# Batched softmax times V: one store a pass out of one result buffer, and the last passes' scores in other parts

## The chip, the cores and the metric

The kernel runs on one core of one Trainium2 chip. The metric is the device time of one execution in microseconds. Before the change three runs gave a median of 1061.16 us (1061.11 to 1061.69).

## What is computed

```python
"scores": np.random.randn(batch, n_heads, seq, seq)      # 8, 12, 1024, 1024, float32
"v":      np.random.randn(batch, n_heads, seq, head_dim) # 8, 12, 1024, 64, float32

scores_max = np.max(scores, axis=-1, keepdims=True)
attn = np.exp(scores - scores_max)
attn = attn / (np.sum(attn, axis=-1, keepdims=True) + 1e-8)
return np.matmul(attn, v)
```

There are 96 heads. For each, 1024 x 1024 scores are turned into weights row by row and multiplied by a 1024 x 64 matrix. The scores are 403 MB, V and the result 25 MB each.

## The kernel before

**Passes.** Four heads make a pass, and 24 passes are one loop (L477). A pass has two halves (`k` = 0 and 1) of two heads each. In a half the 128 partitions hold 2 x 64 groups of 16 consecutive rows of scores: partition x holds rows 0 to 15 of its group, 4 KB a row, so that a half is one [128, 16, 1024] float32 buffer (`s_bufs[k]`, 8 MB), and "a row" below means one row on each of the 128 partitions, 512 KB. V of the four heads is one 1 MB buffer, `v_sb`.

**A row's way.** ScalarE takes the exponential of two rows at a time (L431, one row at a time for the last four of the second half) into one of six `p_nat` buffers, in float16 and without subtracting the maximum. TensorE turns the row in eight 128 x 128 transposes (L444) into PSUM (`psT`, two buffers), VectorE copies two rows (L456, or one, L452) into `pt` (two buffers), and TensorE multiplies with V and a column of ones in eight matmuls (L164), three rows behind the transposes (`LAG`). The order on TensorE is written out by hand (`in_line`): transposes of row r, then products of row r - 3. After every three rows VectorE takes the reciprocal of the column of ones (L143) and multiplies (L151) into `out_bufs[k]`, [128, 16, 64] float32, 512 KB. GpSimd spreads V with ones into `vones` (L289) for each half and copies the finished results of both halves from `out_bufs` into two further buffers, `done` (`put_by`, L182), from which they are stored a pass later. ScalarE also watches V for size (L301), VectorE gathers the smallest and largest sums (L319, L320), and at the very end a judgement (L328 to L340) says whether the sums stayed in range; if not, a slow general path (L342) would do everything anew. With these inputs it isn't taken.

**SyncE's queue.** All transfers of the loop are issued on SyncE, in an order fixed by hand (`queue`). After the last transposes of a pass's first half, `load_first` (L255) issues for the next pass V (L277), the stores of the pass before (`store_before`, L187, one DMA for each half, L193; in passes 0 and 22 their condition is false, and pass 23 takes another branch), and the scores of the first half (L249). These go in one DMA of 8 MB, in the last two loads in parts of 4, 6 and 6 rows. After the whole pass `last` (L386) issues the scores of the second half, one DMA, or in the last two loads parts of 4, 2, 2, 2, 2, 2, 1 and 1 rows. Scores are loaded into the buffer that the same half of the current pass has just freed, so an issue waits on the exponentials that read it. A DMA is also held back until an earlier DMA that counts on the same semaphore has landed. Passes are counted from 0; the loads for passes 22 and 23 are the ones in parts.

**The last results.** There is no pass behind the last to store its results. In the last pass (23), `load_first` stores pass 21 from `done` and pass 22 from V's buffer (`spare`: in pass 22 `put_by` copies there, after V has been read), four DMAs of 512 KB through `store_last` (L206, L210); then `end` (L216) stores the last pass straight from `out_bufs`, in DMAs of 512, 384 and 128 KB, the last one for rows 12 to 15 of the second half.

Of the kernel before, what the change touches and what calls it, by code (L numbers as in the profile page):

```python
# [8 lines left out]
FP32 = mybir.dt.float32  # L9
# [17 lines left out]
def kernel(  # L27
# [6 lines left out]
    nc = tc.nc  # L34
    P = 128

    B, H, SQ, SK = scores.shape
    Bv, Hv, SKv, D = v.shape
    assert (B, H, SK) == (Bv, Hv, SKv)
    BH = B * H  # L40
# [5 lines left out]
    AHEAD = 4  # L46
# [6 lines left out]
    T = 2  # L53
    K = AHEAD // T
    W = P // T
    R = SQ // W
    PASSES = BH // AHEAD
# [8 lines left out]
    out_rows = out.rearrange("b h (j r) d -> (b h j) (r d)", j=W)  # L66

    const_pool = ctx.enter_context(tc.tile_pool(name="const", bufs=1))
    sb_pool = ctx.enter_context(tc.tile_pool(name="sbpool", bufs=1))
# [10 lines left out]
    def buffers(pool, count, shape, dtype, name):  # L80
        return [pool.tile(shape, dtype, name=f"{name}{k}") for k in range(count)]

    s_bufs = buffers(sb_pool, K, [P, R, SK], FP32, "s_nat")
    v_sb = sb_pool.tile([P, C // L, S, L, D], FP32, name="v_sb")
    p_bufs = buffers(sb_pool, 6, [P, EB, SK], FP16, "p_nat")
    pt_bufs = buffers(sb_pool, 2, [P, EB, SK], FP16, "pt")
    out_bufs = buffers(sb_pool, K, [P, R, D], FP32, "out_sb")
    done_bufs = buffers(sb_pool, K, [P, R, D], FP32, "done")
    small_pool = ctx.enter_context(tc.tile_pool(name="small", bufs=1))
    seen = small_pool.tile([P, 1 + K * R + 2], FP32, name="seen")  # L90
    nc.gpsimd.memset(seen, 1.0)
# [1 line left out]


    psO_bufs = buffers(ps_pool, 4, [P, 512], FP32, "psO")
    for buf in done_bufs:
        nc.vector.memset(buf, 0.0)  # L97
    cell = small_pool.tile([P, 1], FP32, name="cell")
    nc.vector.memset(cell, 0.0)
    done = [buf[:].rearrange("x r d -> x (r d)") for buf in done_bufs]  # L100
    spare = [
        v_sb[:].rearrange("x h s l d -> x (h s l d)")[:, k * R * D : (k + 1) * R * D]
        for k in range(K)
    ]
    turn = {}

    def take(bufs):
# [23 lines left out]
    def queue(dma):  # L131

        if queued:
            after(dma, queued[-1])
        queued.append(dma)
# [42 lines left out]
    def put_by(homes):  # L178

        for k in range(K):  # L180
            fills.append(
                nc.gpsimd.tensor_copy(  # L182
                    out=homes[k], in_=out_bufs[k][:].rearrange("x r d -> x (r d)")
                )
            )

    def store_before(m):  # L187

        before = (m + (PASSES - 1)) % PASSES
        for k in range(K):  # L190
            to = out_rows.rearrange("(m x) y -> m x y", x=P)[bass.ds(before * K + k, 1)]
            send(
                nc.sync.dma_start(  # L193
                    out=to.rearrange("o x y -> (o x) y"), in_=done[k], cond=(before < PASSES - 3)
                )
            )

    def send(dma):
        for other in stores:
            apart(dma, other)  # L200
            apart(other, dma)
        apart(dma, dma)
        stores.append(dma)
        queue(dma)

    def store_last(parts):  # L206

        for ago, k, home, a, b in parts:
            n = BH - ago * AHEAD + T * k
            store = nc.sync.dma_start(  # L210
                out=out_rows[n * W : (n + T) * W, a * D : b * D], in_=home[:, a * D : b * D]
            )
            ends.append(store)
            send(store)

    def end():  # L216

        cut = (GROUPS - 2) * G
        left = [out_bufs[k][:].rearrange("x r d -> x (r d)") for k in range(K)]
        store_last(((1, 0, left[0], 0, R), (1, 1, left[1], 0, cut), (1, 1, left[1], cut, R)))  # L220

    stores, fills, ends = [], [], []
    writers, users = {}, {}

    def apart(a, b, reason="stores of two heads are disjoint"):
        tc.declare_no_dep(a.ins, b.ins, across_iterations=True, reason=reason)
# [18 lines left out]
    def load(k, m, parts=(R,), r=0, **cond):  # L245
        rows_n = sc_rows[bass.ds(m * K + k, 1)].rearrange("o x r k -> (o x) r k")
        for rows in parts:
            queue(
                nc.sync.dma_start(  # L249
                    out=s_bufs[k][:, r : r + rows, :], in_=rows_n[:, r : r + rows, :], **cond  # L250
                )
            )
            r += rows

    def load_first(m):  # L255


        before = queued[-1:]
        n = (m + 1) % PASSES
        with tc.If(m < PASSES - 1) as cmp:  # L260
            load_v(n)
            store_before(m)
            then = queued[-1:]
            with tc.If(m < PASSES - 3) as cmp2:
                load(0, n)
            with cmp2.Else():
                queued[:] = then
                load(0, n, (4, 6, 6))
        with cmp.Else():
            queued[:] = before  # L270
            store_last([(3, k, done[k], 0, R) for k in range(K)])
            store_last([(2, k, spare[k], 0, R) for k in range(K)])

    def load_v(m, **cond):

        rows = v_bh.rearrange("(m x) y -> m x y", x=P)
        dma = nc.sync.dma_start(  # L277
            out=v_sb[:].rearrange("x h s l d -> x (h s l d)"),
            in_=rows[bass.ds(m, 1)].rearrange("o x y -> (o x) y"),
            **cond,  # L280
        )
        fills.append(dma)
        queue(dma)

    def spread_v(k):

        for t in range(T):
            for s in range(S):
                op = nc.gpsimd.tensor_copy(  # L289
                    out=vones[s * Q : (s + 1) * Q, k, :, t, 0:D].rearrange(  # L290
                        "i (h l) d -> i h l d", l=L
                    ),
                    in_=v_sb[(k * T + t) * Q : (k * T + t + 1) * Q, :, s],
                )
        return op

    def watch_v():


        junk = p_bufs[-1][:].rearrange("p r k -> p (r k)")  # L300
        return nc.scalar.activation(  # L301
            out=junk,
            in_=v_sb[:].rearrange("p h s l d -> p (h s l d)"),
            func=mybir.ActivationFunctionType.Abs,
            scale=1.0 / SUM_MAX,
            accum_out=seen[:, K * R + 1 : K * R + 2],
        )
# [8 lines left out]
    def fold():  # L316

        n = K * R + 1
        nc.vector.tensor_reduce(out=seen[:, 0:1], in_=seen[:, 0 : n + 1], axis=X, op=ALU.min)  # L319
        nc.vector.tensor_reduce(  # L320
            out=seen[:, n + 1 : n + 2], in_=seen[:, 1 : n + 2], axis=X, op=ALU.max
        )

    def judge(bank):

        n = K * R + 1
        part = small("part")
        nc.vector.tensor_scalar(  # L328
            out=part, in0=seen[:, n + 1 : n + 2], scalar1=1.0, scalar2=None, op0=ALU.is_le
        )  # L330
        nc.vector.scalar_tensor_tensor(  # L331
            out=right, in0=seen[:, 0:1], scalar=1.0 / SUM_MAX, in1=part, op0=ALU.is_ge, op1=ALU.mult
        )
        cell = bank[0:1, G * M : G * M + 1]
        in_line(
            nc.tensor.matmul(  # L336
                out=cell, lhsT=right[:], rhs=vones[:, 0, 0, 0, D : D + 1], start=True, stop=True
            )
        )
        nc.vector.tensor_copy(out=count[:], in_=cell)  # L340
# [45 lines left out]
    def last(m, bank):  # L386

        before = queued[-1:]
        k = K - 1
        with tc.If(m < PASSES - 1) as cmp:  # L390
            spread = spread_v(k)
            watch = watch_v()
            n = (m + 1) % PASSES
            with tc.If(m < PASSES - 3) as cmp2:  # L394
                put_by(done)
                queued[:] = before
                load(k, n)
            with cmp2.Else():
                with tc.If(m < PASSES - 2) as cmp3:
                    put_by(done)  # L400
                with cmp3.Else():
                    gate = nc.gpsimd.tensor_copy(out=cell, in_=out_bufs[k][:, R - 1, D - 1 : D])
                    for op in (watch, spread):
                        tc.add_manual_dep(
                            gate.ins,
                            op.ins.name,
                            mybir.DependencyInfo(
                                mybir.DependencyClass.Sync, mybir.DependencyReason.DATA
                            ),
                            reason="the values have been read",  # L410
                        )
                    put_by(spare)
                queued[:] = before
                load(k, n, (4, 2, 2, 2, 2, 2, 1, 1))
        with cmp.Else():
            queued[:] = before
            end()
            fold()
            judge(bank)

    def heads(m):

        for k in range(K):
            st = dict(psO=[take(psO_bufs) for g in range(GROUPS)])
            for r in range(R):
# [32 lines left out]
                if r == R - 1 and k < K - 1:  # L458
                    load_first(m)
# [58 lines left out]
```

## Time and profile before

| | |
|---|---|
| median of three runs | 1061.16 us (1061.11 to 1061.69) |
| the profiled execution | 1061.0 us |
| its span, first to last instruction | 1057.2 us |
| mean granted clock of TensorE | 0.889 |
| PE / PEld / DVE / ACT / POOL busy | 77 / 74 / 67 / 71 / 27% |
| read from HBM, written to it | 427.82 MB, 27.26 MB |
| chain that ended last | DMA of scores 7% of the span, other steps 1% and less |

PE is TensorE's matmuls, PEld its weight loads, DVE VectorE, ACT ScalarE, POOL GpSimd, SP SyncE; a q behind a name means the engine's sequencer, which issues and waits. A row of the page's groups names line, engine, operation, output and inputs with shapes and count, then busy us and mean ns of one, then idle time of the engine just before and what ended it. A row of a timeline has start in us from the span's start, length in us, engine, line, operation, tiles and count, and in brackets the idle time before. A row of windows has the stretch and its length, then the busy us of PE, PEld, DVE, ACT and POOL with their counts, then the granted clock of TensorE (1.00 is full), the mean busy share of the 16 DMA engines, and GB/s. The share can pass 1 a little, since packets overlap.

### The profile page before, as it was taken

What the parts mean: (1) busy time and instruction counts of PE and PEld (TensorE: products, weight loads), DVE (VectorE), ACT (ScalarE), POOL (GpSimd) and SP (SyncE); (2) the same over time, 40 slices, a digit from 0 to 9 for tenths busy, and PEclk for the clock granted to TensorE, in tenths of its full rate; (3) what the DMA queues carried; (4) which work ended last, traced back from release to release, by engine and by line L of the source; (5) the groups of instructions that cost most, each with busy time, mean ns of one, the idle gap of its engine ahead of it and who ended that gap; (6) DMA issues with size and microseconds to landing.
All of it is one profiled execution on the core that took longest, in us unless ns stands there. A gap on an engine that the chain in (4) does not pass through costs nothing. (4 is left out here: it accounts for less than half of the span.)

```text
span 1057.2 us, 32536 instructions
## 1 busy us (share of the span) xinstructions
PE 814.0 (77%) x12289; PEld 779.1 (74%) x12289; DVE 705.7 (67%) x1352; ACT 749.8 (71%) x482; POOL 286.6 (27%) x447
## 2 busy tenths in 40 slices
PE   3488668786787867878778777887777886878987
PEld 2488668785787867867678767787677876878877
DVE  2377566685676856767567675676656766667878
ACT  4487578776787667876778667786687856878965
POOL 4041231312323124121241221412214123131241
PEclk9799888898888988989889897898988889889999
DMA  9999999999999999999999999999999999999998
GB/s 397 438 437 429 404 454 427 426 431 426 447 436 436 436 431 441 422 436 427 423 435 436 436 436 436 436 436 412 446 434 429 422 430 443 436 436 420 424 429 322
DMA packets 20164, 453.06 MB, mean 429 GB/s; under 512 B 2240, under 2 KB 2368, under 8 KB 9024
## 3 DMA queue, kind: packets, MB, share of 16 engines
q1 hardware_dynamic: 20160, 452.99, 99.7%
q8 instruction: 4, 0.07, 0.0%
HBM read 427.82 MB, written 27.26 MB: 430 GB/s over the span
## 5 line engine op out<-in xcount | busy, mean ns | idle before, releaser
L431 ACT ACTIVATE p_nat<-s_nat 128x2048 f16<-128x2048 f32 (+1 forms) x432 | 702.7, 1711 | 291.6 <-SPq L394 159.6
L444 PE MATMUL psT<-ident,p_nat 128*128 128x128 f16 x6144 | 521.1, 236 | 214.0 <-ACT p_nat L431 212.7
L456 DVE COPY pt<-psT 128x2048 f16<-128x2048 f16 x336 | 411.3, 1224 | 310.3 <-PE L444 151.2
L444 PEld LDWEIGHTS <-p_nat 128*128 128x128 f16 x6144 | 436.5, 120 | 228.6 <-ACT p_nat L431 225.9
L164 PE MATMUL psO<-vones,pt 128*128 128x130 f16 x6144 | 499.1, 227 | 23.9 <-DVE pt L452 10.7
L289 POOL CAST vones<-v_sb 32x512 f16<-32x512 f32 x392 | 239.1, 610 | 761.2 <-PE L444 393.0
L164 PEld LDWEIGHTS <-pt 128*128 128x128 f16 x6144 | 400.6, 101 | 43.9 <-DVE pt L456 24.5
L151 DVE TENSOR_TENSOR out_sb<-psO,seen 64x192 f32<-64x192 f32 (+1 forms) x576 | 192.0, 333 | 22.1
L452 DVE COPY pt<-psT 128x1024 f16<-128x1024 f16 x96 | 63.4, 682 | 1.5
L143 DVE RECIPROCAL seen<-psO 128x3 f32<-128x3 f32 (+1 forms) x288 | 49.7, 173 | 11.9 <-PE L444 7.5
L301 ACT ACTIVATE p_nat<-v_sb 128x2048 f16<-128x2048 f32 x24 | 45.7, 1903 | 0.7 <-DMA v_sb<-in_v_dram 0.7
L182 POOL COPY done<-out_sb 128x1024 f32<-128x1024 f32 x44 | 44.5, 1037 | 4.8 <-issue 4.8
L301 ACT ACT_TABLE_LOAD x1 | 1.3, 1283 | 5.7 <-DMA v_sb<-in_v_dram 5.7
L319 DVE TENSOR_REDUCE seen<-seen 128x1 f32<-128x34 f32 x25 | 4.7, 189 | 0.8
L301 ACT ACTIVATION_READ_ACCUMULATOR p_nat<-v_sb 128x1 f32 x24 | 4.5, 189 | 0.0
L320 DVE TENSOR_REDUCE seen<-seen 128x1 f32<-128x34 f32 x25 | 4.5, 179 | 0.0
L97 DVE MEMSET done<- 128x1024 f32 x2 | 1.8, 912 | 1.2 <-DVEq L477 1.0
L182 POOL COPY v_sb<-out_sb 128x1024 f32<-128x1024 f32 x2 | 2.0, 1040 | 0.0
L336 PE MATMUL psO<-vones,right 128*1 128x1 f16 x1 | 0.2, 164 | 1.7 <-DVE right L331 1.7
L336 PEld LDWEIGHTS <-right 128*1 128x1 f16 x1 | 0.1, 79 | 1.9 <-DVE right L331 1.9
L340 DVE CAST count<-psO 1x1 int32<-1x1 f32 x1 | 0.1, 146 | 0.3 <-PE psO L336 0.3
masks.py:199 POOL TENSOR_SCALAR_AFFINE_SELECT ident<-ident 128x128 f32<-128x128 f32 x1 | 0.3, 295 | 0.1
(12 smaller groups left out, 1.8 us busy)
## 6 DMA issues: line engine op xcount, KB each, us to landing
v_sb<-in_v_dram SPq DMA_DIRECT2D x24, 1024.0 KB, 17.0
out_dram<-done SPq DMA_DIRECT2D x48, 512.0 KB, 12.0
s_nat<-in_scores_dram SPq DMA_DIRECT2D x4, 3072.0 KB, 24.4
s_nat<-in_scores_dram SPq DMA_DIRECT2D x10, 1024.0 KB, 27.7
s_nat<-in_scores_dram SPq DMA_DIRECT2D x2, 4096.0 KB, 18.7
s_nat<-in_scores_dram SPq DMA_DIRECT2D x4, 2048.0 KB, 23.3
s_nat<-in_scores_dram SPq DMA_DIRECT2D x4, 512.0 KB, 23.0
out_dram<-v_sb SPq DMA_DIRECT2D x2, 512.0 KB, 7.8
```

Source lines behind the costliest of these rows:

```text
L143: nc.vector.reciprocal(out=recip, in_=psO[:, :, D : D + 1])
L151: norm = nc.vector.tensor_tensor(out=out_bufs[k][part, g * G : g * G + rows, :], in0=psO[part, :, t * N : t * N + D], in1=recip[part].to_b ...
L164: product = nc.tensor.matmul(out=st["psO"][g][:, i * M : (i + 1) * M], lhsT=pt[:, c * P : (c + 1) * P], rhs=vones[:, k, c].rearrange("p t ...
L182: nc.gpsimd.tensor_copy(out=homes[k], in_=out_bufs[k][:].rearrange("x r d -> x (r d)"))
L289: op = nc.gpsimd.tensor_copy(out=vones[s * Q : (s + 1) * Q, k, :, t, 0:D].rearrange("i (h l) d -> i h l d", l=L), in_=v_sb[(k * T + t) * Q ...
L301: return nc.scalar.activation(out=junk, in_=v_sb[:].rearrange("p h s l d -> p (h s l d)"), func=mybir.ActivationFunctionType.Abs, scale=1. ...
L319: nc.vector.tensor_reduce(out=seen[:, 0:1], in_=seen[:, 0 : n + 1], axis=X, op=ALU.min)
L320: nc.vector.tensor_reduce(out=seen[:, n + 1 : n + 2], in_=seen[:, 1 : n + 2], axis=X, op=ALU.max)
L431: exp = nc.scalar.activation(out=p_nat[:, g : g + rows, :].rearrange("p r (x v) -> p x r v", v=Q * L), in_=s_bufs[k][:, r + g : r + g + ro ...
L444: turned = nc.tensor.transpose(out=psT[:, c * P : (c + 1) * P], in_=p_row[:, c // L, c % L, :], identity=ident16[:],)
L452: copy = nc.vector.tensor_copy(out=pt, in_=psT)
L456: copy = nc.vector.tensor_copy(out=pt2[:], in_=psT2[:])
```

## The change

The two `done` buffers become one tile, [128, 2, 1024] float32; GpSimd's copies go to its two halves, and a pass's results leave by one DMA of 1 MB that names for each partition two pieces of 4 KB, one in each half's rows of the result. The copies of pass 22 into V's buffer are addressed in the same manner. In the last pass the results of passes 21 and 22 leave by one DMA each instead of two; the three stores of the last pass stay as they are. The scores of the first half for passes 22 and 23 come in parts of 8, 4 and 4 rows, those of the second half in 4, 4, 2, 2, 2, 1 and 1. The description of the change adds that SyncE's program then has 187 words.

```diff
-    done_bufs = buffers(sb_pool, K, [P, R, D], FP32, "done")
+    done = sb_pool.tile([P, K, R * D], FP32, name="done")
...
-    for buf in done_bufs:
-        nc.vector.memset(buf, 0.0)
+    for k in range(K):
+        nc.vector.memset(done[:, k], 0.0)
...
-    done = [buf[:].rearrange("x r d -> x (r d)") for buf in done_bufs]
-    spare = [
-        v_sb[:].rearrange("x h s l d -> x (h s l d)")[:, k * R * D : (k + 1) * R * D]
-        for k in range(K)
-    ]
+    spare = v_sb[:].rearrange("x h s l d -> x (h s l d)").rearrange("x (k y) -> x k y", k=K)
...
-                    out=homes[k], in_=out_bufs[k][:].rearrange("x r d -> x (r d)")
+                    out=homes[:, k], in_=out_bufs[k][:].rearrange("x r d -> x (r d)")
...
+    def of_pass(m):
+
+        rows = out_rows.rearrange("(m k x) y -> m x k y", k=K, x=P)
+        return rows[bass.ds(m, 1)].rearrange("o x k y -> (o x) k y")
+
     def store_before(m):
 
         before = (m + (PASSES - 1)) % PASSES
-        for k in range(K):
-            to = out_rows.rearrange("(m x) y -> m x y", x=P)[bass.ds(before * K + k, 1)]
-            send(
-                nc.sync.dma_start(
-                    out=to.rearrange("o x y -> (o x) y"), in_=done[k], cond=(before < PASSES - 3)
-                )
-            )
+        send(nc.sync.dma_start(out=of_pass(before), in_=done[:], cond=(before < PASSES - 3)))
...
-    def store_last(parts):
-
-        for ago, k, home, a, b in parts:
-            n = BH - ago * AHEAD + T * k
-            store = nc.sync.dma_start(
-                out=out_rows[n * W : (n + T) * W, a * D : b * D], in_=home[:, a * D : b * D]
-            )
-            ends.append(store)
-            send(store)
+    def store_last(to, rows):
+        store = nc.sync.dma_start(out=to, in_=rows)
+        ends.append(store)
+        send(store)
...
-        left = [out_bufs[k][:].rearrange("x r d -> x (r d)") for k in range(K)]
-        store_last(((1, 0, left[0], 0, R), (1, 1, left[1], 0, cut), (1, 1, left[1], cut, R)))
+        for k, a, b in ((0, 0, R), (1, 0, cut), (1, cut, R)):
+            n = BH - AHEAD + T * k
+            store_last(
+                out_rows[n * W : (n + T) * W, a * D : b * D],
+                out_bufs[k][:, a:b, :].rearrange("x r d -> x (r d)"),
+            )
...
-                load(0, n, (4, 6, 6))
+                load(0, n, (8, 4, 4))
...
-            store_last([(3, k, done[k], 0, R) for k in range(K)])
-            store_last([(2, k, spare[k], 0, R) for k in range(K)])
+            store_last(of_pass(PASSES - 3), done[:])
+            store_last(of_pass(PASSES - 2), spare)
...
-                load(k, n, (4, 2, 2, 2, 2, 2, 1, 1))
+                load(k, n, (4, 4, 2, 2, 2, 1, 1))
```

## The prediction

> **What bounds the kernel now.** I read the page first: time, DMA, queues.
>
> ```profile
> span 1057.2 us, 32536 instructions
> ...
> DMA packets 20164, 453.06 MB, mean 429 GB/s; under 512 B 2240, under 2 KB 2368, under 8 KB 9024
> ...
> q1 hardware_dynamic: 20160, 452.99, 99.7%
> q8 instruction: 4, 0.07, 0.0%
> ```
>
> The 16 DMA engines are taken 99.7% of the span, while no compute engine of the page passes 77%. The 2240 packets under 512 B are 16 for each of 140 landed DMAs: each DMA ends with one small packet per engine. Then the stretches that no first or last pass touches, in windows, and the issues of two passes on SyncE:
>
> ```profile
> 104.00:940.00 836.00, 652.17 (x9786) 624.49 (x9783) 561.12 (x1077) 592.10 (x380) 225.80 (x346) 0.88 1.00 433
> ```
>
> ```profile
> 204.69 0.33 SPq L277 DMA_DIRECT2D v_sb<-in_v_dram  x1
> ...
> 859.51 0.33 SPq L277 DMA_DIRECT2D v_sb<-in_v_dram  x1
> ```
>
> Share 1.00 over 836 us: the transfers never stop. The two loads of V are 15 passes apart, so a pass takes 654.82 / 15 = 43.65 us. It moves 2 x 8.389 MB of scores, 1.049 MB of V and 1.049 MB of results, 18.87 MB.
>
> So only the end can bend. There, the timelines of ScalarE, TensorE and SyncE over the last pass:
>
> ```profile
> 1011.64 3.72 ACT L431 ACTIVATE p_nat<-s_nat 128x2048 f16<-128x2048 f32 x2 [2.91 <-PE psT L444]
> 1018.89 5.52 ACT L431 ACTIVATE p_nat<-s_nat 128x2048 f16<-128x2048 f32 x3 [3.53 <-PE L164]
> 1026.12 16.56 ACT L431 ACTIVATE p_nat<-s_nat 128x2048 f16<-128x2048 f32 x9 [1.72 <-DMA s_nat<-in_scores_dram]
> 1043.93 3.91 ACT L431 ACTIVATE p_nat<-s_nat 128x1024 f16<-128x1024 f32 x4 [1.24 <-PE L444]
> ```
>
> ```profile
> 1014.42 0.63 PE L164 MATMUL psO<-vones,pt 128*128 128x130 f16 x8 [0.45 <-DVE pt L452]
> 1016.21 1.95 PE L444 MATMUL psT<-ident,p_nat 128*128 128x128 f16 x32 [1.15 <-DVE out_sb L151]
> 1018.74 0.62 PE L164 MATMUL psO<-vones,pt 128*128 128x130 f16 x8 [0.58 <-DVE pt L456]
> 1020.86 0.64 PE L444 MATMUL psT<-ident,p_nat 128*128 128x128 f16 x8 [1.50 <-ACT p_nat L431]
> 1021.33 0.92 PE L164 MATMUL psO<-vones,pt 128*128 128x130 f16 x8
> ...
> 1028.09 0.64 PE L444 MATMUL psT<-ident,p_nat 128*128 128x128 f16 x8
> ...
> 1043.81 0.39 PE L444 MATMUL psT<-ident,p_nat 128*128 128x128 f16 x4
> ```
>
> ```profile
> 994.51 0.33 SPq L277 DMA_DIRECT2D v_sb<-in_v_dram  x1
> 996.88 2.56 SPq L193 DMA_DIRECT2D out_dram<-done  x2
> 1001.85 24.62 SPq L249 DMA_DIRECT2D s_nat<-in_scores_dram  x11
> 1035.93 2.75 SPq L210 DMA_DIRECT2D out_dram<-done  x2
> 1040.88 3.32 SPq L210 DMA_DIRECT2D out_dram<-v_sb  x2
> 1047.09 5.88 SPq L210 DMA_DIRECT2D out_dram<-out_sb  x3
> ```
>
> ScalarE starts at 1011.64, 1018.89 and 1026.12: the first half's parts of 4, 6 and 6 rows (2, 3 and 3 exponentials) arriving. The starts are 7.25 and 7.23 us apart, 6 rows each: **1.207 us a row**, 524288 B / 1.207 = 434.4 GB/s, so the first two are landings as well, whatever releaser the row names. From 1026.12 on nothing of the first half is missing, and the question is who is late. The windows with the granted clock:
>
> ```profile
> 1014.66:1018.07 3.41, 2.26 (x39) 2.04 (x36) 1.86 (x6) 0.69 (x1) 2.62 (x5) 1.00 0.99 425
> 1018.07:1021.49 3.42, 1.35 (x21) 1.11 (x20) 1.65 (x2) 2.60 (x2) 3.11 (x6) 1.00 1.07 460
> 1021.49:1024.90 3.41, 3.41 (x36) 3.41 (x33) 1.65 (x3) 2.92 (x2) 1.31 (x2) 0.50 0.93 401
> ...
> 1028.09:1051.73 23.64, 22.64 (x377) 21.52 (x376) 22.14 (x44) 18.41 (x12) 3.37 (x6) 1.00 0.97 389
> ```
>
> TensorE is busy 22.64 of the last 23.64 us, so **from row 10 of the first half on TensorE, with VectorE's copies, sets the end**, and the last data is not late: the last exponential ends at 1047.84, the last products only at 1051.7. From the transposes of row 10 at 1028.09 to those of row 26 at 1043.81 are 16 rows in 15.72 us, **0.98 us a row** against DMA's 1.207.
>
> **The change, part by part.** All against the profiled execution: 1061.0 us, 3.8 us of it outside the span. The median of the runs is 1061.16.
>
> *One store for two.* In passes 1 to 21 the two stores of 512 KB become one of 1 MB, at the end four become two, and the last scores' parts fall from 11 to 10 in two passes: 21 + 2 + 2 = 25 DMAs fewer, the same bytes. What a DMA costs by itself: at 434.4 GB/s a pass's 18.87 MB take 43.44 us of its 43.65, so all five DMAs of a pass together cost 0.21 us at most. A fifth of it, 0.04 us, is my upper guess for the average, 25 x 0.04 = 1.0 us; the lower end is 0. I take 0.3, nearer to none, since the bytes and most packets stay. If the second store alone carried all 0.21 us, the end would be 21 x 0.21 = 4.4 us earlier. It could also lose: a partition now reads two 4 KB pieces and writes them far apart; no row has such a store, and I bound that loss by the same 1.0 us. The second issue that goes from SyncE is hidden: its queue waits on the exponentials in any case (504 us below), and the copies into the buffer (two of 1.04 us on GpSimd) end long before the issue.
>
> *Counters and waits.* SyncE's waits:
>
> ```profile
> SPq L249 <- ACT p_nat L431: 504.3, 50, 26.4
> ...
> SPq L277 <- DMA s_nat<-in_scores_dram: 5.3, 1, 5.3
> ...
> SPq L193 <- DMA s_nat<-in_scores_dram: 3.5, 2, 1.9
> ```
>
> A load of V that waits 5.3 us for scores has no data reason: it shares a landing counter with an earlier part. Eight counters taken in turn by program order fit this. With one store and one part fewer, the counter of pass 22's V load passes from the part of rows 6 and 7 to that of rows 10 and 11, 4 x 1.207 = 4.8 us later, so it issues at 994.5 + 4.8 = 999.3. Behind it on SyncE stand the skipped store and all scores of the last pass. The work that hides it is DMA's own queue: V lands at 1018.89 - 10 x 1.207 = 1006.8, the last row of pass 22 (1.049 MB / 434.4 GB/s = 2.4 us) before it, at 1004.4, the last but one at 1003.2. With this last but one row's counter the first scores are issued at 1003.2 instead of 1001.85, 3.6 us before V is through. Once this cover is gone, each us late is a us lost.
>
> *Parts of 8, 4, 4.* Pass 22's scores: ScalarE is still busy with pass 21 when the 8 rows land, nothing moves. Last pass: the first exponential waits for 8 rows instead of 4, 1011.64 + 4 x 1.207 = 1016.47, less 0.3: 1016.2. It ends 1.90 later, at 1018.1; the following pairs end every (5.52 - 1.90) / 2 = 1.81 us, without the waits of 3.53 and 1.72. Rows 4 and 5 are ready at 1018.1 + 2 x 1.81 = 1021.7, and from there TensorE needs 0.98 a row: row 10 at 1027.6 (its exponential: 1018.1 + 5 x 1.81 = 1027.2, in time). Before it was 1028.09, so **0.5 us earlier, if the clock stays up**.
>
> It will hardly stay. In the window 1018.07 to 1021.49 TensorE was busy 1.35 of 3.42 us and the next window ran at clock 0.50; there a group of eight takes about 0.85 instead of 0.45 (1022.05 to 1022.90 the transposes). After the change TensorE has nothing from 1015.05 (1014.42 + 0.63) to 1018.1, then two rows, then waits again: a window that holds this is emptier still. If the slow window falls on 1018.07 to 1021.49, the first four rows end at 1021.6 and row 4 begins at 1022.05: 0.35 late, row 10 at 1028.0, 0.1 before now. If it begins near 1019.9, it holds 3.4 us of full work, which fills half the rows: up to 1.6 late, row 10 at 1029.2, 1.1 after now. The middle, 0.8 late, gives row 10 at 1028.4, **0.3 us later than now**. Before, the slow window lay ahead of ScalarE's gap of 1.72 us, which swallowed it; now there is no gap behind it. The Trainium skill ("TensorE: Matmul & The Clock Gate", Part 1: The HAM clock gate) says that about 3.4 us of idling put the array on half clock and about 3.4 us of work bring it back, in windows that run free of the program; these rows agree (3.41 us at 0.50), and without such a rule the part would be worth the 0.5 us.
>
> *Parts of 4, 4, 2, 2, 2, 1, 1.* Rows 4 and 5 of the second half now land with rows 6 and 7: 1026.12 + 8 x 1.207 - 0.3 = 1035.5, exponential done at 1037.4. TensorE comes to row 20 at 1028.4 + 10 x 0.98 = 1038.2: hidden by its backlog; if that went, at most 0.5 us appear.
>
> *The end.* After the last products come normalising, the judging and the last store, which all move with TensorE:
>
> ```profile
> L210 SPq DMA_DIRECT2D out_dram<-out_sb x3: 332/333/336, 1047.1 to 1052.6; - x3
> ```
>
> ```profile
> DMA to landing us min/median/max: 1.9/5.8/12.0
> ```
>
> Issued at 1052.6, landed 1.9 later, at 1054.5, with 2.7 us of closing behind. The merged stores of `done` and V's buffer queue behind the last scores as now, so DMA itself would be through some 0.3 us earlier, but the last store waits for VectorE. An end earlier by more than 0.7 us would meet the stores before it.
>
> *Words of SyncE.* Instruction packets by the DMA view of 24 to 60 us, and of 1056 us to the end:
>
> ```profile
> q8 instruction: 3, 0.05, 0.5%
> ```
>
> ```profile
> q8 instruction: 1, 0.02, 4.6%
> ```
>
> Three between 24 and 60 us, when SyncE stands in its longest wait (26.4 us) and TensorE goes through its long body for the first time, and one after 1056. So none of the three is SyncE's as I read them; the fourth comes after the last landing. I take 0; bounds 0 to 0.9 us gained (4.6% of 16 engines over 1.2 us).
>
> Sum: 1061.0 + 0.3 = **1061.3 us**.
>
> **The rivals.**
>
> 1. *The clock stays up or the data wins.* Row 10 0.5 us earlier, DMA saving up to 1.0 instead of 0.3: 1061.0 - 0.5 - 0.7 = 1059.8 at the far end, 1060.5 by the values taken. For it: ScalarE loses two gaps. Against: the idle stretch of 3 us.
> 2. *Slower: the clock stays down for two windows.* The mean clock of 0.88 over the middle puts (1 - 0.88) / 0.5 = 0.24 of every pass, 10 us or three windows, at 0.50. Two windows of 3.41 us, begun near 1019.9, hold rows 2 to 6 with their products; row 7 starts 2.9 us late, row 10 at 1030.5 against 1028.09: 2.4 later, 1063.4. Begun at 1018.07 they cost 1.3, 1062.3. It decides only if the first slow window finds too little work. Against: before, one busy window was enough to come back.
> 3. *Each store has a price of its own.* Then 21 of them go: at most 4.4 us by the rows, 1056.6. Against: share 1.00 and 433 GB/s with stores, 434.4 without. The Trainium skill ("DMA: Bandwidth & Descriptors", Rules for kernel authors and Anatomy of one DMA) asks for 1 MiB or more per DMA and fits a fixed cost of about 2.0 us each on another issuing path; by that 25 DMAs would be worth 50 us, an estimate from that page; the pass length here leaves no room for it.
> 4. *It does nothing.* The parts of the last pass are lost in TensorE's backlog and the stores in a full queue: 1061.0.
>
> **How the numbers follow.** A measurement of this kernel can tell about 0.2%, 2.1 us, from no change. Forecast 0.60 (1060.9 to 1062.1); rival 1 0.17, of it 0.05 beyond the bound by a dearer store; rival 2 0.13, of it 0.08 beyond, with the far loss of a store in two pieces added; rival 3 0.02; rival 4 0.08. Faster 0.05 + 0.02 = 0.07, slower 0.08, rounded up to 0.09 for what the counters may do, within 0.84. The range takes rival 1's far end and rival 2's: 1059.8 to 1063.4.
>
> **What would show it.** In the page after: 25 x 16 = 400 packets under 512 B fewer, a mean still near 429 GB/s. In ScalarE's timeline: one start near 1016.2 and no gap until the second half's data. In the windows: a stretch of clock 0.50 beginning between 1017 and 1020. Row 10's transposes near 1028.4, the last products about 0.3 after 1051.7. I am wrong if the pass is not 43.6 us, if the first scores of the last pass are issued after V has landed, or if the last products end with a gap of TensorE ahead of them.

## The result, and the profile after

The changed kernel took 1059.38 us (median of 22 runs, 1059.06 to 1059.73), the kernel before 1061.07 us (22 runs, 1060.39 to 1061.69). The ratio is 0.9985, with a 95% interval of 0.9979 to 0.9990: some 1.7 us faster, below the range of the prediction. The profiled execution took 1059.14 us.

First the page of after: span, packets, queues and the chain that ended last.

```profile
span 1057.4 us, 32323 instructions
...
DMA packets 19508, 453.06 MB, mean 428 GB/s; under 512 B 1840, under 2 KB 1968, under 8 KB 8624
...
q1 hardware_dynamic: 19504, 452.99, 99.6%
q8 instruction: 4, 0.07, 0.0%
...
PEld 3%; DVE 2%; PE 1%; POOL 0%; issue 0%; ACT 0%; PEldq 0%; POOLq 0%; ACTq 0%
```

**The span has not become shorter**: 1057.4 us against 1057.2. What became shorter is what lies outside it: 1061.0 - 1057.2 = 3.8 us before, 1059.14 - 1057.4 = 1.74 us after. The single runs say the same. Over the 22 runs of after the time outside the span is 1.79 us (1.71 to 1.88), over the 30 runs of before that stand beside the first four experiments 3.91 us (3.40 to 4.21). The span's median is 1057.6 (1057.3 to 1058.0) against 1057.15 (1056.9 to 1057.5). So the change **gains 2.1 us outside the span and loses 0.45 us inside it**.

What runs behind the span shows when a window of the DMA view is put there. Before, from 1057.2 to 1063 us (the second row is queue, packets, MB, share of 16 engines):

```profile
DMA packets 2, 0.02 MB, mean 3 GB/s; under 512 B 0, under 2 KB 0, under 8 KB 0
...
q14 instruction: 2, 0.02, 0.9%
```

After, from 1057.4 to 1063 us:

```profile
DMA packets 0, 0.00 MB, mean 0 GB/s; under 512 B 0, under 2 KB 0, under 8 KB 0
```

Before, two instruction packets of 8 KB come on queue 14 when every instruction that the trace shows has ended; by the trace's records they start at 1058.62 and 1060.80 us. After, none comes.

Inside the span, ScalarE's last pass (timeline of after; start, length, then the tiles, and in brackets the idle time before):

```profile
1016.04 18.33 ACT L425 ACTIVATE p_nat<-s_nat 128x2048 f16<-128x2048 f32 x10 [7.66 <-PE psO L160]
1035.45 9.40 ACT L425 ACTIVATE p_nat<-s_nat 128x2048 f16<-128x2048 f32 x6 [1.08 <-PE psT L438]
1045.15 1.06 ACT L425 ACTIVATE p_nat<-s_nat 128x1024 f16<-128x1024 f32 x1 [0.29 <-PE L438]
1046.66 1.06 ACT L425 ACTIVATE p_nat<-s_nat 128x1024 f16<-128x1024 f32 x1 [0.45 <-PE psT L438]
```

TensorE's timeline of after, with row 10 of the first half and the last products:

```profile
1018.00 1.08 PE L438 MATMUL psT<-ident,p_nat 128*128 128x128 f16 x16 [2.06 <-ACT p_nat L425]
1019.80 1.89 PE L438 MATMUL psT<-ident,p_nat 128*128 128x128 f16 x16 [0.72 <-ACT p_nat L425]
...
1028.08 0.61 PE L438 MATMUL psT<-ident,p_nat 128*128 128x128 f16 x8
...
1051.22 0.63 PE L160 MATMUL psO<-vones,pt 128*128 128x130 f16 x8 [0.45 <-DVE pt L446]
```

And the windows of after, with the granted clock in the third column from the right:

```profile
1014.66:1018.07 3.41, 0.90 (x13) 0.55 (x11) 2.00 (x7) 2.03 (x2) 1.81 (x3) 1.00 1.00 428
1018.07:1021.49 3.42, 2.70 (x32) 2.55 (x33) 1.23 (x1) 3.42 (x3) 3.05 (x5) 0.67 1.00 426
1021.49:1024.90 3.41, 3.41 (x53) 3.41 (x52) 2.00 (x2) 3.41 (x3) 2.15 (x3) 0.83 1.00 428
...
1028.09:1051.73 23.64, 22.43 (x379) 21.43 (x376) 22.14 (x44) 17.65 (x12) 2.25 (x4) 1.00 0.97 394
```

One exponential start replaces three, at 1016.04. The clock is down for (1 - 0.67) x 2 x 3.42 + (1 - 0.83) x 2 x 3.41 = 3.4 us, one stretch begun near 1019.2. Row 10 comes at 1028.08 and the last products at 1051.22, 0.12 later than before. The chain of before had shown no GpSimd at its end. In after GpSimd closes it (chain of after, its last pieces; start, length, what):

```profile
1048.48 0.82 PE psO L160 x15
1049.31 0.59 POOL vones L283
...
1053.98 0.61 POOL vones L283
```

These eight casts spread V into `vones` for a pass that doesn't exist; nobody reads their values. The row names TensorE's products as what released them, but the products that read this half of `vones` (the first half's) ended near 1037.1, some 12 us earlier, and the row of before names the transposes: what ends the wait is a landing. The POOL timelines of before, then of after:

```profile
1048.06 5.29 POOL L289 CAST vones<-v_sb 32x512 f16<-32x512 f32 x8 [25.26 <-PE L444]
```

```profile
1049.30 5.29 POOL L283 CAST vones<-v_sb 32x512 f16<-32x512 f32 x8 [25.64 <-PE psO L160]
```

The first store of `done` in the last pass stands in SyncE's order where other passes have the load of V, and by that order counts on the same landing counter. The DMA view at its issue (engine, KB, us from issue to landing), before with the issue at 1035.93, then after with the issue at 1040.42:

```profile
out_dram<-done SPq DMA_DIRECT2D x1, 512.0 KB, 12.0
```

```profile
out_dram<-done SPq DMA_DIRECT2D x1, 1024.0 KB, 8.7
```

1035.93 + 12.0 = 1047.9 and 1040.42 + 8.7 = 1049.1: in both kernels the casts begin within 0.2 us of that landing, and so they do in all twelve profiles (0.15 us behind it each time, by the trace's own times). The merged store is twice as long, lands 1.2 us later, and the casts end at 1053.98 + 0.61 = 1054.6 instead of some 1053.4.

### The profile page after: what moved, and what is told of

It is laid out like the page before. It is cut to its first block, busy times and chain, and to the rows that moved or that the text cites. A ratio compares the mean times of both kernels' runs of the same rounds, so it can differ in the third digit from the quotient of the medians.

```text
span 1057.4 us, 32323 instructions
## 1 busy us (share of the span) xinstructions
PE 814.7 (77%) x12289; PEld 779.7 (74%) x12289; DVE 705.6 (67%) x1352; ACT 749.6 (71%) x482; POOL 285.5 (27%) x447
```

## The experiments

Three theories. **Theory 1**: the time behind the span goes by the length of SyncE's program, whatever of it is carried out. Counted in the built programs (words of 64 B, branch labels left out) before has 206 words and after the 187 that the change names. The words of the other engines' programs were not counted. **Theory 2**, the rival: it goes by what is carried out, the 25 DMAs fewer or the other parts. **Theory 3**, for the span: the loss comes from GpSimd's casts, which wait for a longer store; its rival is TensorE's clock under parts of 8, 4, 4. All ratios are to before, with a 95% interval. Before had a median of 1061.05, 1061.11 and 1061.08 us beside the first four runs, the next four and the last two.

**Longer again, nothing more carried out.** Four scores loads stand in the loop of the general path, which these inputs never enter:

```diff
 # after, in the loop of general()
+            nc.sync.dma_start(out=s_bufs[0][:, 5, :], in_=s_rows[...])   # four times
```

> The changed kernel, with four loads on SyncE added to the general path, which is not entered with these inputs: every instruction that is executed stays, SyncE's program grows from 187 to 208 words (before the change 206). Theory 1, the gain is the length of SyncE's program, paid after the last instruction: the time outside the span goes back from about 1.8 to 3.8 us, the total from 1059.4 to about 1061.4, the span stays at 1057.6, and two 8 KB instruction packets appear behind the span. Theory 2, the gain is in what is executed (one store, fewer DMAs to close): outside the span 1.8 us, total 1059.4.

1061.57 us (10 runs), ratio 1.0006 (0.9996 to 1.0015): the whole gain is gone. The span is 1057.6 as in after, and 3.90 us (3.82 to 4.22) lie outside it. From 1057 to 1064 us the DMA view shows the two packets of queue 14 again (one of queue 8 comes near the end of every kernel here, changed or not):

```profile
q8 instruction: 1, 0.02, 1.0%
q14 instruction: 2, 0.02, 0.9%
```

Instructions that never run cost 2.1 us. That is theory 1, and theory 2 has no place for it.

The same profile also bears on theory 3. It carries out what after carries out, but TensorE is ahead in it:

```profile
1049.49 5.28 POOL L283 CAST vones<-v_sb 32x512 f16<-32x512 f32 x8 [26.90 <-PE psO L160]
```

```profile
1027.58 0.61 PE L442 MATMUL psT<-ident,p_nat 128*128 128x128 f16 x8
...
1050.73 0.63 PE L160 MATMUL psO<-vones,pt 128*128 128x130 f16 x8 [0.45 <-DVE pt L450]
```

Row 10 and the last products are 0.5 us earlier than in after, the last store lands at 1054.35 instead of 1054.62, and yet the span is 0.2 us longer: the casts began 0.2 us later. Here they alone hold the end.

**Shorter, all DMAs kept.** The kernel before without its general path, with 187 words on SyncE; every store and load of before is carried out. It leaves out the answer to sums out of range, and the branch that asks for it.

```diff
 # before
-    with tc.If(good < P, preferred_fallthrough_block=False):
-        general()
```

> The kernel before the change, with its stores and parts, but without the general path, so that a judgement of out of range would have no consequence; SyncE's program shrinks from 206 to 187 words, what is executed stays but for the jump over the path. Theory 1 (length of SyncE's program): outside the span 1.8 instead of 3.8 us, total about 1059.1. Theory 2 (what is executed, stores and DMAs): nothing gained, 3.8 us and 1061.1.

1058.38 us (9 runs), ratio 0.9975 (0.9965 to 0.9985). Outside the span 1.92 us (1.74 to 2.11); the span is 1056.5, some 0.6 shorter: the last store lands as before (1054.44 against 1054.51), and 2.1 us follow it instead of 2.7, with the branch gone. Without a single DMA less, the 2 us come.

**The new parts alone**, with the two stores of before:

```diff
 # before
-                load(0, n, (4, 6, 6))
+                load(0, n, (8, 4, 4))
...
-                load(k, n, (4, 2, 2, 2, 2, 2, 1, 1))
+                load(k, n, (4, 4, 2, 2, 2, 1, 1))
```

> The kernel before with the new parts of the last passes alone; two stores out of two buffers stay. SyncE's program has 195 words. Theory 1: the threshold lies somewhere from 188 to 206 words, so outside the span either 1.8 or 3.8 us and nothing between, which narrows it; span 1057.2 to 1057.7. Theory 2 (one store for two is what pays): 3.8 us and about 1061.3.

1059.86 us (10 runs), ratio 0.9988 (0.9978 to 0.9997). SyncE has 195 words, and 1.80 us lie outside the span: the parts alone already bring the program below the step. But the span is 1058.05, above the 1057.2 to 1057.7 expected and the longest median of all, and its runs scatter from 1057.0 to 1059.2.

**The change with the old first parts:**

```diff
 # after
-                load(0, n, (8, 4, 4))
+                load(0, n, (4, 6, 6))
```

> The changed kernel with the first half's parts of passes 22 and 23 back at 4, 6 and 6 rows; SyncE's program keeps its 187 words. If the forecast's step on the parts holds (8, 4, 4 costs some 0.3 us because TensorE's slow window has no gap behind it to swallow it), the span is 0.2 to 0.5 us shorter than the changed kernel's, about 1057.2, and the total about 1059.0. If the parts do nothing: 1059.4. If 8, 4, 4 is a gain: 1059.7 or more.

1059.27 us (10 runs), ratio 0.9984 (0.9974 to 0.9994); 187 words, 1.77 us outside, span 1057.45 (1057.3 to 1057.9). The span is 0.15 shorter than after's 1057.6, less than the 0.2 to 0.5 expected: with 8, 4, 4 taken away GpSimd is still there, its casts begin at 1049.31.

**The last store of `done` in two again**, for theory 3:

```diff
 # after
-            store_last(of_pass(PASSES - 3), done[:])
+            for k in range(K):
+                store_last(of_pass(PASSES - 3)[:, k], done[:, k])
```

> The changed kernel, but in the last pass alone the results of pass 21 leave by two stores of 512 KB again; 189 words on SyncE. Theory 3: the span's 0.4 us over the kernel before come from GpSimd, whose eight last casts (5.3 us, of V that nobody reads) wait for the first store of the last pass to land; 1 MB lands at 1049.2, 512 KB about 1.25 us earlier. By it the casts start near 1048.0, GpSimd is done at 1053.7 instead of 1054.9, the end falls back to the last store's landing, the span is 0.2 to 0.4 us shorter (about 1057.2), the total 1059.0 to 1059.2. If the 0.4 us come from the slow clock behind the first part of 8 rows, casts move and the span stays at 1057.6.

1059.55 us (10 runs), ratio 0.9985 (0.9976 to 0.9995), span 1057.75, from 1056.9 to 1059.5. The casts do move:

```profile
1048.66 5.29 POOL L284 CAST vones<-v_sb 32x512 f16<-32x512 f32 x8 [24.44 <-PE psT L439]
```

They begin 0.64 earlier than in after, though the last scores land 0.6 later in this execution (1047.19 against 1046.57); yet the median of the span isn't shorter. In the profiled execution TensorE was on half clock for two windows:

```profile
1018.07:1021.49 3.42, 2.13 (x26) 1.97 (x27) 1.22 (x1) 3.42 (x3) 3.12 (x6) 0.73 1.01 431
1021.49:1024.90 3.41, 3.41 (x35) 3.41 (x33) 1.23 (x1) 3.41 (x3) 2.60 (x4) 0.50 1.00 428
1024.90:1028.31 3.41, 3.41 (x50) 3.41 (x48) 2.23 (x5) 3.41 (x3) 0.00 (x0) 0.77 1.03 442
```

At half speed it spent 0.27 x 2 x 3.42 + 3.41 + 0.23 x 2 x 3.41 = 6.8 us, each window's lost share taken twice. Its rows:

```profile
1030.10 0.61 PE L439 MATMUL psT<-ident,p_nat 128*128 128x128 f16 x8
...
1053.28 0.64 PE L160 MATMUL psO<-vones,pt 128*128 128x130 f16 x8 [0.45 <-DVE pt L447]
```

Row 10 is 2.0 us later than before, the last products 2.2, the span 1059.2. Theory 3 is right about the casts, but alone it doesn't set the span.

**Both at once**, the split store and the old first parts (the two edits above together):

> As the split store, with the first half's parts at 4, 6 and 6 rows as before; 189 words. In the run with these parts alone the last store landed 0.4 us earlier than in the changed kernel, and only GpSimd's casts held the end. Theory 3: both gains add up, span 1056.7 to 1057.0, total 1058.5 to 1058.8, the fastest of all with the general path. If the parts do nothing: as the split store alone.

1059.02 us (10 runs), ratio 0.9979 (0.9969 to 0.9989), span 1057.2 (1056.7 to 1057.6). Against the version with the old first parts alone the casts begin 0.6 earlier and the span's median is 0.25 shorter, not quite the 1056.7 to 1057.0 expected.

**Where the step lies.** Three loads that are never carried out instead of four, 203 words:

> The changed kernel with three never executed loads on SyncE in the general path: 203 words. Theory 1: a threshold between 195 (fast) and 206 (slow); here either 1.8 us outside the span and 1059.4, or 3.9 us and 1061.5, nothing between.

1061.35 us (8 runs), ratio 1.0001 (0.9991 to 1.0011). Outside the span 3.44 us (3.29 to 3.56), between the two levels where nothing was expected, and one packet behind the span (DMA view, 1058.3 to 1064 us):

```profile
DMA packets 1, 0.01 MB, mean 1 GB/s; under 512 B 0, under 2 KB 0, under 8 KB 0
...
q14 instruction: 1, 0.01, 0.4%
```

**The one store alone**, all parts as before, 198 words:

```diff
 # after
-                load(0, n, (8, 4, 4))
+                load(0, n, (4, 6, 6))
...
-                load(k, n, (4, 4, 2, 2, 2, 1, 1))
+                load(k, n, (4, 2, 2, 2, 2, 2, 1, 1))
```

> The changed kernel with all the old parts (4, 6, 6 and 4, 2, 2, 2, 2, 2, 1, 1), so that one store for two is the only change; 198 words. Theory 1: 1.8 us outside the span if the threshold is above 198, else 3.9. Theory 3: the span is that of the changed kernel with old first parts, 1057.5, for the casts wait for the same 1 MB store; total 1059.3 or 1061.4.

1058.89 us (10 runs), ratio 0.9979 (0.9970 to 0.9989). Outside 1.79 us, no packet there; so 198 words are short enough. The span is 1057.05 (1056.9 to 1057.9), 0.25 below that of before beside it (1057.3), and 0.55 below the whole change: better than expected. The single runs of this version and of before overlap, so the 0.25 us is a small difference of medians.

**The one store alone, split again at the end**, 199 words:

> The change with all the old parts (4, 6, 6 and 4, 2, 2, 2, 2, 2, 1, 1) and with the last pass's store of done as two DMAs again; SyncE has 199 words. Theory 1 (length of SyncE's program, with the step between 198 and 203 words): time outside the span 1.8 us if the step lies above 199, 3.4 if it lies at 199. Theory 3 (GpSimd's casts of the last pass wait for the landing of the first store of done): casts start some 0.4 us earlier than in the version that only has the one store, 1048.1 against 1048.5; the span is shorter by at most 0.2 us than its 1057.05, since there the last store's landing already holds the end: 1056.9, time 1058.7. Rival: the split costs as much as it gives, time 1058.9 as in that version.

1058.75 us (11 runs), ratio 0.9979 (0.9970 to 0.9988), span 1057.0 (1056.6 to 1057.4), 1.78 us outside. The casts begin at 1047.89 instead of 1048.51, the span is the same within 0.1: here the last store ends last anyway, as expected. So there are two steps, one packet each: between 199 and 203 words, worth 1.65 us, and between 203 and 206, worth 0.45. It is the fastest version that keeps the general path, though the one before it isn't told apart from it.

**The first parts 8, 4, 4 with the old second parts**, 198 words:

```diff
 # after
-                load(k, n, (4, 4, 2, 2, 2, 1, 1))
+                load(k, n, (4, 2, 2, 2, 2, 2, 1, 1))
```

> The change with the old parts of the second half (4, 2, 2, 2, 2, 2, 1, 1) and the new parts of the first half (8, 4, 4); SyncE has 198 words, so time outside the span 1.8 us by theory 1. What it tells apart is where the 0.5 us of the span come from that the whole change has more (1057.6) than the version with the one store alone (1057.05). If 8, 4, 4 bring them (TensorE's half clock placed late), the span is 1057.4 to 1058 and scatters by a us or more, time 1059.2 to 1059.8. If 4, 4, 2, 2, 2, 1, 1 bring them (last scores issued later, first store of done landed later, GpSimd later), the span is 1057.0, time 1058.9.

1059.68 us (11 runs), ratio 0.9982 (0.9973 to 0.9991), 1.81 us outside, as expected if 8, 4, 4 cost the 0.5 us. The span is 1057.9 and falls in two groups: 1056.4, 1056.5, 1056.9 and 1057.1, and seven runs from 1057.5 to 1058.1. The profiled execution, one of 1058.1, in windows and in TensorE's timeline:

```profile
1014.66:1018.07 3.41, 0.42 (x8) 0.24 (x5) 1.18 (x5) 1.70 (x1) 2.60 (x5) 0.91 1.01 432
1018.07:1021.49 3.42, 3.15 (x29) 2.98 (x30) 1.22 (x1) 3.42 (x3) 3.11 (x6) 0.50 1.04 446
1021.49:1024.90 3.41, 3.41 (x40) 3.41 (x38) 1.23 (x2) 3.41 (x3) 1.31 (x2) 0.59 0.95 408
```

```profile
1018.34 3.70 PE L438 MATMUL psT<-ident,p_nat 128*128 128x128 f16 x32 [3.25 <-ACT p_nat L425]
...
1029.00 0.61 PE L438 MATMUL psT<-ident,p_nat 128*128 128x128 f16 x8
...
1052.15 0.64 PE L160 MATMUL psO<-vones,pt 128*128 128x130 f16 x8 [0.45 <-DVE pt L446]
```

The parts of 8, 4, 4 make TensorE idle 3.25 us, the clock is down for two windows (6.8 us), row 10 is 0.9 later and the last products 1.05 later than before. The same stretch in the version with the old parts and the split store:

```profile
1018.07:1021.49 3.42, 1.39 (x22) 1.25 (x23) 1.55 (x2) 2.73 (x2) 3.11 (x6) 1.00 1.03 446
1021.49:1024.90 3.41, 3.41 (x64) 3.41 (x62) 2.35 (x5) 2.79 (x2) 1.20 (x2) 1.00 1.00 430
```

There the clock stays up in this execution; in before it was down for one window, ahead of a gap of ScalarE that swallowed it.

**What decides between one slow window and two.** The clock's records in the traces change in steps of 3.41 us, and their edges lie elsewhere from execution to execution. With windows on these edges, first after, then the change with the last store in two again:

```profile
1015.81:1019.22 3.41, 1.22 (x19) 0.93 (x16) 0.95 (x5) 3.18 (x2) 2.89 (x5) 1.00 1.04 447
1019.22:1022.63 3.41, 2.83 (x27) 2.83 (x28) 2.09 (x2) 3.41 (x3) 3.10 (x7) 0.50 0.97 418
1022.63:1026.05 3.42, 3.42 (x63) 3.42 (x61) 2.12 (x5) 3.42 (x3) 1.03 (x2) 1.00 1.02 436
```

```profile
1016.23:1019.64 3.41, 1.25 (x21) 1.01 (x18) 1.01 (x5) 2.96 (x2) 2.76 (x5) 1.00 1.00 428
1019.64:1023.05 3.41, 2.69 (x27) 2.60 (x26) 1.89 (x2) 3.41 (x3) 3.10 (x6) 0.50 1.00 428
1023.05:1026.47 3.42, 3.42 (x35) 3.42 (x33) 1.21 (x2) 3.42 (x3) 1.17 (x2) 0.50 1.05 450
```

TensorE was busy 2.83 us of the slow window in the one, and the clock came back; 2.69 in the other, and it stayed down. The other kernels with 8, 4, 4 fit: one slow window with 3.08 us of work in it (208 words), two where the first held 2.65 (the new parts alone), 2.55 (8, 4, 4 with the old second parts) or none (203 words). Over all windows of the twelve traces up to 1050 us, the clock fell after 499 windows with at most 1.64 us of TensorE's work and stayed up after 2326 with at least 1.45; it came back after 487 with at least 2.64 and stayed down after 322 with at most 2.70. So in these traces it falls below some 1.5 us of work in 3.41 and returns above some 2.7; which side a stretch lands on depends on where the window's edges lie.

**What ends the span.** The last store's landing and the end of the casts can be set against the end of the span in every profile. In four kernels, after and those with 208 words, with 203 words and with the old first parts, the span ends 2.79 or 2.80 us after the casts, and the last store's landing lies 2.75 to 3.21 us before the end. In the seven others with the general path it ends 2.57 to 2.68 us after that landing, and the casts end 3.1 us or more before the end. The four are those whose first store is merged and whose second half comes in 4, 4, 2, 2, 2, 1, 1. In after itself the two are nearly level, so there the casts hold the end by 0.2 us at most. The chain alone would not show this: in the version with the one store alone it closes in the casts too, though the last store lands 0.5 us after them.

## Why the prediction was wrong, point by point

**The step that failed: "Words of SyncE"**, "I take 0; bounds 0 to 0.9 us gained", together with the 3.8 us outside the span, which went into the sum unchanged. The runs put 2.1 us there: before 3.9, after 1.8, and over all versions the time follows the number of words (206 and 208 words 3.9; 203 words 3.44; 199, 198, 195, 189 and 187 words 1.8 to 1.9), also between after and the versions of 203 and 208 words, which carry out the same. The bound was taken from a packet of queue 8, which is there before and after. The view that the prediction shows ends with the span; the two packets of queue 14 stand just behind it.

The Trainium skill ("Runtime: NRT & Kernel Launch", Instruction fetch mechanics) says that a sequencer fetches its program in blocks of 16 KiB, 256 instructions, and that crossing a block is mostly hidden. The three packets of queue 8 ahead of 60 us fit that size; the step here doesn't follow from it: the packets have 8 KB, come when nothing is left to hide them, and the steps lie between 199 and 206 words. Which fetch these packets are is open; that they go with the program's length is shown.

**The span itself** was forecast at 1057.2 + 0.3 = 1057.5 us and is 1057.4 in the profile, 1057.6 in the median. That the number fits is luck in part, since the prediction's 0.3 us were TensorE's, and in after TensorE's last products are only 0.12 us later. Term by term:

- *One store for two*: 0.3 us were taken for DMA, within 0 to 1.0, and none of it at the end. The page shows exactly the 400 packets under 512 B fewer. V lands 653.8 us apart over 15 passes in both traces, so the pass is unchanged at 43.59 us (the 43.65 of the prediction came from issues, which shift; with 43.59 its bound for all DMAs of a pass is 0.15 us, not 0.21). The two versions with the one store and the old parts have spans 0.25 and 0.2 us below those of before beside them: near the size taken, though the prediction had let none of it reach the end. That DMA gave it isn't shown: the profiles of both also have the clock up where before's was down. Rival 3, a price for every store, is out.
- *"The merged stores of `done` and V's buffer queue behind the last scores as now"*: not as now. The longer first store lands 1.2 us later and GpSimd's useless casts wait for it. The prediction followed the last store to VectorE, but never asked who else counts on the landing that the merge moves. In after the casts hold the end, by little; with the old first parts, splitting that store again shortens the span by 0.25 us.
- *Counters*: V's load of pass 22 was expected at 999.3, the first scores at 1003.2, all hidden. SyncE's timeline of after:

```profile
999.02 0.33 SPq L271 DMA_DIRECT2D v_sb<-in_v_dram  x1
...
1002.67 18.56 SPq L243 DMA_DIRECT2D s_nat<-in_scores_dram  x10
...
1047.11 5.99 SPq L202 DMA_DIRECT2D out_dram<-out_sb  x3
```

  Right, and the last scores' landing moves by 0.03 us (1046.57 against 1046.60).
- *Parts of 8, 4, 4*: first exponential 1016.2 expected, 1016.04 measured; row 10 1028.4 expected between 1028.0 and 1029.2, 1028.08 measured. Right as a range, and 0.3 us late as a middle. Over all kernels with these parts it is a matter of where the clock's windows fall: row 10 at 1027.58, 1028.08, 1028.62, 1029.00, 1029.23 and 1030.10 in the six profiles. The prediction went by a rule of idling; before's window ahead of the fall had 1.35 us of work in it, so an idle window isn't needed. And with parts of 4, 6, 6 the clock fell in three of six profiles and stayed up in three: before's slow window is itself an accident of the execution.
- *Rival 2, two slow windows*, was given 0.13 with spans of 1058.5 to 1059.6 (its 1062.3 to 1063.4 less 3.8). Four of the six profiles with 8, 4, 4 show it, at 1058.1, 1058.3, 1058.5 and 1059.2. The mechanism was right, with its condition that the first slow window finds too little work; the price was up to 0.4 us high (row 10 came 0.5 to 2.0 us later than before, not 1.3 to 2.4), and the chance, by these profiles, too low. Whether some runs of after had two windows can't be told from their spans (1057.3 to 1058.0). *Rival 1's* row 10 half a us earlier is what the version with 208 words shows, 1027.58, with the clock down for one window that began early; the casts then kept the end. That the four short spans of the last experiment are of this kind is argued, as none was profiled.
- *Parts of 4, 4, 2, 2, 2, 1, 1*: hidden by TensorE's backlog as expected; ScalarE starts them at 1035.45 against a forecast of 1035.5. But the casts hold the end only where these parts and the merged store come together: with the one store and the old first parts the median of the span is 1057.45, with all the old parts 1057.05.

**What stays open**: what in SyncE's program, or in how it is fetched, puts the steps between 199 and 206 words; how much of the span's 0.45 us is GpSimd's and how much the clock's in after's unprofiled runs. A last pass without GpSimd's casts wasn't tried, nor the parts of the second half without the rest.

## What to carry to other kernels

The time of a run less its span is a term of its own: look at the DMA view behind the last instruction, and where instruction packets come there, count the words of the engines' programs (here SyncE's mattered; of the others no run tells); an edit that shortens one can gain 2 us without touching the work. Before two transfers are merged, ask who waits for the landing of the first of them, in the last pass too, where a counter may release work that nobody needs. A gap that is closed in a tail is no gain if the work that is left bunches up behind an idle stretch and meets a slow clock, and it is none either while another engine's last work holds the end.

## What was not expected of the hardware

Code that is never carried out cost time: four load instructions in a loop that isn't entered cost 2.1 us of a 1060 us run, as 8 KB packets behind the last instruction. The cost comes in steps, not per word: 19 words fewer on before gave 2.0 us, while 187 to 199 words are all alike within 0.15 us.

In these traces TensorE's clock goes down after a window of 3.41 us with less than some 1.5 us of its work in it, idle or not, and comes back only after one with more than some 2.7 us: 0.14 us of work, 2.83 against 2.69, decided between one slow window and two.
